# Issuing the first load ahead of the program's opening barrier in a ReLU-and-row-sum kernel

## The chip, the cores and the metric

The kernel runs on one core of one Trainium2 chip. The metric is the device time of one execution in microseconds (us), as the median of several runs. "The span" is the time from the first to the last instruction of the profiled execution; it is shorter than the measured time of the same execution, by 1.66 us in the profiled run of the kernel before (162.37 - 160.71). SyncE issues all loads and stores, ACT is the scalar engine, DVE the vector engine, POOL is GpSimd. A load's issue is SyncE's instruction that starts it; its lead is the time from the start of the issue to its first packet of data; it has landed when its semaphore has its full count.

The time before the change was 162.47 us (three runs, 162.46 to 162.50).

## The reference

```python
x = np.random.randn(32, 512, 1024).astype(np.float32)   # batch, seq, dim

def reference(x):
    relu_x = np.maximum(x, 0)
    return np.sum(relu_x, axis=-1).astype(np.float32)
```

The kernel reads 67.1 MB once, and writes 16,384 sums (0.07 MB).

## The kernel before

The rows are spread over 128 partitions, 128 rows of 1024 numbers on each. Seven big loads ("chunks") of 16 rows for each partition (8.39 MB) go in turn into three buffers, followed by a tail of smaller loads. SyncE issues the first three loads at once and each later one when DVE has finished with its buffer. ACT applies ReLU in place, and DVE sums.

```python
    sp, act, dve = nc.sync, nc.scalar, nc.vector

    tb = NBIG % NB                       # NBIG = 7 chunks, NB = 3 buffers
    for c in range(NBIG + 1):
        if c >= NB:
            sp.wait_ge(s_dve, 3 * (c - NB + 1))
        if c < NBIG:
            g, j = CHUNKS[c]
            sp.dma_start(out=buf[:, c % NB, :, :], in_=xv[g][:, j : j + BIG, :]).then_inc(
                s_in[c], 16
            )
    # ... the tail: loads of 8, 4, 2, 1/2 and 1/2 rows for each partition; the big store ...

    for c in range(NTWO):                # NTWO = 6 chunks are computed so
        b, steps = c % NB, STEPS if c < NTWO - 1 else MIXED
        act.wait_ge(s_in[c], 16)
        # ... two rows of the sixth chunk on DVE alone ...
        for i, n in enumerate(steps):    # STEPS = 4, 5 and 7 rows
            t = buf[:, b, r : r + n, :]
            act.activation(t, t, AF.Relu).then_inc(s_act, 1)
            dve.wait_ge(s_act, 3 * c + i + 1)
            dve.tensor_reduce(
                out=res[:, c * BIG + r : c * BIG + r + n], in_=t, axis=X, op=ALU.add
            ).then_inc(s_dve, 1)
            r += n
    # ... the last chunk and the tail, row by row on ACT and DVE; the small store ...
```

None of this is the first thing that the program does. The framework puts an opening before it: POOL fills four small constants, the four other engines announce their arrival at a barrier (a `DRAIN` instruction that increments one semaphore), and POOL, when it has reached its own `DRAIN` behind the constants, waits for these four arrivals and releases all by a second semaphore. In SyncE's stream of instructions the arrival and the wait for the release stand ahead of the first load.

## Time and profile before

| quantity | value | where it stands |
|---|---|---|
| time, span | 162.47 us, 160.7 us | runs, page |
| share of the load queue in 16 DMA engines' time | 97.4% | page, part 3 |
| busy DVE, ACT | 76%, 63% of the span | page, part 1 |
| first load issued | 0.73 us | timeline |
| first ReLU starts (load 0 has landed) | 22.61 us | timeline |
| second ReLU of a new chunk starts | 41.94 us, 19.33 us later | timeline |

Lines of the profile's page of the kernel before: the busy times of the engines, the DMA queue (packets, MB, share of the time of 16 engines) and the traffic with HBM.

```profile
span 160.7 us, 145 instructions
DVE 122.0 (76%) x56; ACT 101.0 (63%) x55; POOL 0.2 (0%) x4
...
q1 hardware_dynamic: 2160, 67.18, 97.4%
HBM read 67.11 MB, written 0.07 MB: 418 GB/s over the span
```

No compute engine is near full (76% and 63%), and the DMA engines are (97.4%). The waits of the kernel before say the same: who waited, for whom, and for how long (total us, times, longest).

```profile
ACT buf L118 <- DMA buf<-in_x_dram: 47.1, 6, 20.6
DVE res L120 <- ACT buf L118: 34.3, 10, 26.3
ACT buf L98 <- DMA buf<-in_x_dram: 9.7, 5, 6.6
```

ACT waits for data and DVE waits for ACT. Chunks follow each other at 19.33 us, or 8.39 MB / 19.33 us = 434 GB/s.

The timeline of the kernel before, its first 46 us (start, duration, engine, line, operation; in brackets the idle time before it and what ended that). "SPq L72 ... x4" merges the issues of loads 0 to 3, so its 43.92 us are the stretch from the first to the fourth.

```profile
0.23 0.10 POOL L169 MEMSET const-float32-0.0<- 128x1 f32 x1 [0.23 <-issue]
...
0.72 1.28 ACT L118 ACT_TABLE_LOAD   x1 [0.72 <-PEq L169]
0.73 43.92 SPq L72 DMA_DIRECT2D buf<-in_x_dram  x4
22.61 14.04 ACT L118 ACTIVATE buf<-buf 128x4096 f32<-128x4096 f32 x3 [20.60 <-DMA buf<-in_x_dram]
26.25 9.85 DVE L120 TENSOR_REDUCE res<-buf 128x4 f32<-128x4096 f32 x2 [26.25 <-ACT buf L118]
...
41.94 7.97 ACT L118 ACTIVATE buf<-buf 128x4096 f32<-128x4096 f32 x2 [5.29 <-DMA buf<-in_x_dram]
```

No load is issued until 0.73 us. The merged views leave the barrier out, since its instructions are not counted as work. The trace's single records have them (ns from the span's start, duration, engine):

```
   0    7  SyncE   DRAIN             arrival at the barrier
 304  181  POOL    DRAIN             its own, behind the four constants
 529   17  POOL    EVENT_SEMAPHORE   four arrivals are in
 607   17  POOL    EVENT_SEMAPHORE   release
 649   17  SyncE   EVENT_SEMAPHORE   passes
 731  383  SyncE   DMA_DIRECT2D      issue of load 0
1165  427  SyncE   DMA_DIRECT2D      issue of load 1
1751       DMA     first packet of data
```

SyncE arrives first of all engines and then does nothing for 0.65 us. It waits for POOL, whose own `DRAIN` ends at 0.49 us: POOL's records start at 0.14 us, and its four constants, which load 0 doesn't use, take from 0.24 to 0.44 us.

### The profile page before, as it was taken

What the parts mean: (1) busy time and instruction counts of PE and PEld (TensorE: products, weight loads), DVE (VectorE), ACT (ScalarE), POOL (GpSimd) and SP (SyncE); (2) the same over time, 40 slices, a digit from 0 to 9 for tenths busy, and PEclk for the clock granted to TensorE, in tenths of its full rate; (3) what the DMA queues carried; (4) which work ended last, traced back from release to release, by engine and by line L of the source; (5) the groups of instructions that cost most, each with busy time, mean ns of one, the idle gap of its engine ahead of it and who ended that gap; (6) DMA issues with size and microseconds to landing.
All of it is one profiled execution on the core that took longest, in us unless ns stands there. A gap on an engine that the chain in (4) does not pass through costs nothing.

```text
span 160.7 us, 145 instructions
## 1 busy us (share of the span) xinstructions
DVE 122.0 (76%) x56; ACT 101.0 (63%) x55; POOL 0.2 (0%) x4
## 2 busy tenths in 40 slices
DVE  0000004998969898898969989699899999598995
ACT  3000039991599907997099951999329980496972
POOL 0000000000000000000000000000000000000000
DMA  8969969969969969969969969969969969899993
GB/s 261 522 261 522 522 261 522 522 261 522 522 261 522 522 261 522 522 261 522 522 261 522 522 261 522 522 261 522 522 261 522 506 277 522 367 416 391 418 399 113
DMA packets 2160, 67.18 MB, mean 418 GB/s; under 512 B 496, under 2 KB 496, under 8 KB 880
## 3 DMA queue, kind: packets, MB, share of 16 engines
q1 hardware_dynamic: 2160, 67.18, 97.4%
HBM read 67.11 MB, written 0.07 MB: 418 GB/s over the span
## 4 chain that ended last, share of the span: by engine, by line
DMA 69%; ACT 18%; DVE 10%; SPq 1%; issue 0%
DMA buf<-in_x_dram 69%; ACT buf L118 17%; DVE res L120 9%; SPq L78 1%; ACT buf L98 0%; DVE last L101 0%; SPq L72 0%
## 5 line engine op out<-in xcount | busy, mean ns | idle before, releaser
L120 DVE TENSOR_REDUCE res<-buf 128x4 f32<-128x4096 f32 (+3 forms) x18 | 100.4, 5604 | 34.3 <-ACT buf L118 34.3
L118 ACT ACTIVATE buf<-buf 128x4096 f32<-128x4096 f32 (+3 forms) x18 | 80.8, 4553 | 47.1 <-DMA buf<-in_x_dram 47.1
L98 ACT ACTIVATE buf<-buf 128x1024 f32<-128x1024 f32 (+1 forms) x18 | 18.4, 1021 | 9.7 <-DMA buf<-in_x_dram 9.7
L101 DVE TENSOR_SCALAR_CACHE_REDUCE buf<-buf 128x1024 f32<-128x1024 f32 x18 | 21.0, 1215 | 2.7 <-DMA buf<-in_x_dram 2.5
L98 ACT ACTIVATION_READ_ACCUMULATOR buf<-buf 128x1 f32 x18 | 3.4, 186 | 0.0
L118 ACT ACT_TABLE_LOAD x1 | 1.3, 1283 | 0.7 <-PEq L169 0.7
L101 DVE DVE_READ_ACCUMULATOR buf<-buf 128x1 f32 x18 | 1.5, 83 | 0.0
L101 DVE TENSOR_SCALAR_CACHE_REDUCE last<-last 128x513 f32<-128x513 f32 x1 | 0.7, 690 | 0.2 <-ACT buf L98 0.2
L169 POOL MEMSET const-bfloat16-1.0<- 128x1 bf16 x1 | 0.1, 102 | 0.0
L169 POOL MEMSET const-uint8-127<- 128x1 uint8 x1 | 0.1, 102 | 0.0
L169 POOL MEMSET const-float32-0.0<- 128x1 f32 x1 | 0.1, 99 | 0.2 <-issue 0.2
L169 POOL MEMSET const-float32-1.0<- 128x1 f32 x1 | 0.1, 99 | 0.0
L101 DVE DVE_READ_ACCUMULATOR last<-last 128x1 f32 x1 | 0.1, 83 | 0.0
## 6 DMA issues: line engine op xcount, KB each, us to landing
buf<-in_x_dram SPq DMA_DIRECT2D x1, 4096.0 KB, 26.7
buf<-in_x_dram SPq DMA_DIRECT2D x1, 2048.0 KB, 31.2
buf<-in_x_dram SPq DMA_DIRECT2D x1, 1024.0 KB, 33.2
buf<-in_x_dram SPq DMA_DIRECT2D x1, 512.0 KB, 34.0
buf<-in_x_dram SPq DMA_DIRECT2D x1, 256.0 KB, 34.2
last<-in_x_dram SPq DMA_DIRECT2D x1, 256.0 KB, 34.3
buf<-in_x_dram SPq DMA_DIRECT2D x7, 36.3
out_dram<-res SPq DMA_DIRECT2D x1, 56.0 KB, 10.6
```

The lines of the kernel that those rows point to most:

```text
L78: sp.dma_start(out=buf[:, tb, r : r + n, :], in_=xv[-1][:, r : r + n, :]).then_inc(s_in[NBIG + i], 16)
L98: return act.activation(t, t, AF.Relu, accum_out=acc)
L101: return dve.tensor_scalar(out=t, in0=t, scalar1=0.0, scalar2=None, op0=ALU.max, op1=ALU.add, accum_out=acc)
L118: act.activation(t, t, AF.Relu).then_inc(s_act, 1)
L120: dve.tensor_reduce(out=res[:, c * BIG + r : c * BIG + r + n], in_=t, axis=X, op=ALU.add).then_inc(s_dve, 1)
L169: nc = _bacc.Bacc("TRN2", target_bir_lowering=False, num_devices=1)
```

## The change

The intent is to start the load stream at once. The instruction that issues load 0 is built as before, and then taken from the end of the instruction list and put ahead of SyncE's arrival. It writes one buffer and one semaphore that nothing ahead of the barrier touches, and the output is correct.

```diff
     tb = NBIG % NB
+    code = nc.main_func.blocks[0].instructions
+    arrival = next(
+        i
+        for i, ins in enumerate(code)
+        if ins.engine == mybir.EngineType.SP and type(ins).__name__ == "InstDrain"
+    )
     for c in range(NBIG + 1):
         # ... as before ...
             sp.dma_start(out=buf[:, c % NB, :, :], in_=xv[g][:, j : j + BIG, :]).then_inc(
                 s_in[c], 16
             )
+        if c == 0:
+            code.insert(arrival, code.pop())
```

## The prediction

> **What bounds the kernel now.** The load stream. The page gives queue 1 a 97.4% share of the span (67.11 MB read, 418 GB/s over the span). In the DMA packet records data packets run from 1.75 us to 157.92 us without a gap. The landings of the big loads are 19.35 us apart (8.39 MB each, 433 GB/s, worked out). The vector engine (76% busy) and the scalar engine (63%) wait for data: 47.1 + 9.7 us and 34.3 us in the table of waits. The chain of waits (DMA 69%) also walks through ACT and DVE, which release buffers, but that release is not tight: load 3 is issued when chunk 0 is reduced at 44.3 us, while load 2 lands only at about 61 us, so some 17 us of work is always queued. So what moves the stream's start moves every landing equally, and the end (last landing, 157.7 us, two short operations, the small store) follows.
>
> **What the change removes, adds, moves.** Before, in the timeline, SyncE's arrival at the barrier is the first instruction of the span (0.00 us, 7 ns). GpSimd's four memsets and its own arrival end near 0.49 us, GpSimd gathers at 0.53 and releases at 0.61, SyncE passes at 0.65, and the first load's issue starts at 0.73 us (383 ns long). Its first packet starts 1.02 us after that issue starts. The barrier thus stands wholly ahead of the stream. After the change the issue takes the place of the arrival, at about 0.00 to 0.06 us, and the first packet should start near 1.05 us of the same clock. Gain at the start: 0.67 to 0.73 us.
>
> **What it costs elsewhere.** SyncE reaches the barrier about 0.43 to 0.50 us later. GpSimd gathers at 0.53 us anyhow, so the release moves by 0 to 0.1 us. Behind it stand the table load of ACT (1.28 us, needed only at 22 us) and loads 1 and 2, which have about 19 us of slack behind load 0. So this costs nothing. [...]three loads being issued 0.43 to 0.48 us apart. So the arrival after the load should not wait for 8 MB.
>
> **Predicted time.** Nearly the whole gain survives, since the stream has no idle time that could absorb it: 162.47 - 0.69 = 161.78 us, 0.4% faster, so "same" at 2%. Range 161.6 to 162.05 us. Faster by over 2%: 0.005; within 2%: 0.99; slower by over 2%: 0.005.
>
> **What the profile would show.** First load's issue at about 0.0 us; the first landing's consumer (the first ACT activation, now 22.61 us) at about 21.9 us; activations still 19.35 us apart; the span near 160.0 us; loads 1 and 2 issued at about 0.7 to 0.8 and 1.2 us, not after 20 us.
>
> **What would make it wrong.** (a) The arrival waits until the load's data has landed: then load 1 is issued after 22 us, the stream has a hole of about 1 us, and the time is unchanged or up to 0.5 us worse. (b) The first issue is slower when it comes straight after the launch, which eats part of the 0.69 us. (c) The measured time, which is 1.7 us longer than the span, starts where the first instruction does and hides part of the gain.

## The result, and the profile after

| | before | after | difference |
|---|---|---|---|
| time, median (6 runs each) | 162.47 us | 161.53 us | 0.94 us |
| range of the runs | 162.19 to 162.53 | 161.42 to 161.65 | |
| span of the profiled run | 160.71 us | 159.91 us | 0.80 us |

The ratio is 0.9947, with a 95% interval of 0.9934 to 0.9960. Ratios in this document are the mean time of one kernel's runs over the mean of the other's in the same rounds, so not quite the ratio of the medians: here the means differ by 0.865 us and the medians by 0.94.

The page of the changed kernel, the same lines (line numbers in the source moved by 8 to 10):

```profile
span 159.9 us, 145 instructions
DVE 122.0 (76%) x56; ACT 101.0 (63%) x55; POOL 0.2 (0%) x4
...
q1 hardware_dynamic: 2160, 67.18, 97.9%
HBM read 67.11 MB, written 0.07 MB: 420 GB/s over the span
```

The work is the same to the tenth of a us; only the share of the queue rose, because the stretch without data at the start is shorter (1.01 us against 1.75). The waits of the changed kernel:

```profile
ACT buf L128 <- DMA buf<-in_x_dram: 46.3, 6, 19.7
DVE res L130 <- ACT buf L128: 33.5, 10, 25.5
ACT buf L108 <- DMA buf<-in_x_dram: 9.7, 5, 6.6
```

ACT's waits for data shrank by 0.8 us, DVE's for ACT by 0.8 us, and the longest wait of each, the one for chunk 0, gave all of it (20.6 to 19.7 and 26.3 to 25.5, rounded). The timeline of the changed kernel, its first 46 us:

```profile
0.00 43.86 SPq L80 DMA_DIRECT2D buf<-in_x_dram  x4
...
0.79 1.28 ACT L128 ACT_TABLE_LOAD   x1 [0.79 <-PEq L179]
21.82 14.04 ACT L128 ACTIVATE buf<-buf 128x4096 f32<-128x4096 f32 x3 [19.75 <-DMA buf<-in_x_dram]
25.46 9.85 DVE L130 TENSOR_REDUCE res<-buf 128x4 f32<-128x4096 f32 x2 [25.46 <-ACT buf L128]
...
41.13 7.98 ACT L128 ACTIVATE buf<-buf 128x4096 f32<-128x4096 f32 x2 [5.27 <-DMA buf<-in_x_dram]
```

Load 0 is issued at 0.00. ACT's table load, which stands behind the barrier, starts 0.06 us later than before (0.786 against 0.725 us in the single records). Everything from the first ReLU on is 0.8 us earlier, at the same spacing. The single records of the changed kernel's opening:

```
   0  383  SyncE   DMA_DIRECT2D      issue of load 0
 300  181  POOL    DRAIN
 431  132  SyncE   DRAIN             arrival (7 ns long before the change)
 589   17  POOL    EVENT_SEMAPHORE   four arrivals are in
 667   17  POOL    EVENT_SEMAPHORE   release
 709   17  SyncE   EVENT_SEMAPHORE   passes
 791  332  SyncE   DMA_DIRECT2D      issue of load 1
1010       DMA     first packet of data
```

The first packet comes 0.741 us sooner (1.751 to 1.010), and each of the thirteen loads lands 0.79 to 0.82 us sooner, load 0 included. So the gain is complete when load 0 has landed and nothing of it is lost over the 138 us that follow. What is to be settled is whether the earlier start is really the whole cause, whether the barrier still costs anything, and what the difference between 0.73 (the issue), 0.80 (the span) and 0.94 us (the medians) is.

### The profile page after: what moved, and what is told of

The parts are those of the page before. It is cut to its first block, busy times and chain, and to the rows that moved or that the text cites. A ratio compares the mean times of both kernels' runs of the same rounds, so it can differ in the third digit from the quotient of the medians.

```text
span 159.9 us, 145 instructions
## 1 busy us (share of the span) xinstructions
DVE 122.0 (76%) x56; ACT 101.0 (63%) x55; POOL 0.2 (0%) x4
## 4 chain that ended last, share of the span: by engine, by line
DMA 69%; ACT 18%; DVE 10%; SPq 1%; issue 0%
DMA buf<-in_x_dram 69%; ACT buf L128 18%; DVE res L130 10%; SPq L88 1%; ACT buf L108 0%; DVE last L111 0%
## 5 line engine op out<-in xcount | busy, mean ns | idle before, releaser
L130 DVE TENSOR_REDUCE res<-buf 128x4 f32<-128x4096 f32 (+3 forms) x18 | 100.4, 5604 | 33.5 <-ACT buf L128 33.5
```

Source lines behind the costliest of these rows:

```text
L130: dve.tensor_reduce(out=res[:, c * BIG + r : c * BIG + r + n], in_=t, axis=X, op=ALU.add).then_inc(s_dve, 1)
```

## The experiments

The theory is: time = time of the first load's issue + a constant. Rivals are that the late release of the barrier costs a part (or its lateness matters elsewhere), that any early DMA would do because the first one warms something up, that the landing of load 0 and not the stream counts, and that part of the 0.94 us is scatter. The variants of one call ran on one chip, beside runs of the kernel before on the same chip.

### Once more, and a third time: how large is the gain?

The edit is none; the changed kernel was timed again.

> The changed kernel once more, timed in more rounds beside its variants. Theory (the stream starts about 0.74 us earlier, nothing else counts): 0.65 to 0.90 us below the kernel before, so a ratio near 0.995; span about 159.9 us. Rival (part of the 0.94 us between the two medians of the first result is scatter between runs): nearer 0.75 than 0.94 us. If the gain is well over 0.85 us, something besides the earlier start is faster too.

> The changed kernel a third time, beside the two others on one chip: a ratio of 0.995 to 0.996 to the kernel before, 0.65 to 0.90 us.

| | before, mean (runs) | changed, mean (runs) | gain | ratio, 95% interval |
|---|---|---|---|---|
| the first result | 162.40 us (6) | 161.54 us (6) | 0.865 us | 0.9947 (0.9934 to 0.9960) |
| again | 162.28 us (9) | 161.62 us (5) | 0.661 us | 0.9960 (0.9947 to 0.9972) |
| third | 162.29 us (11) | 161.52 us (6) | 0.768 us | 0.9955 (0.9940 to 0.9969) |

Over all runs the means are 162.31 us (26 runs) and 161.56 us (17 runs), a gain of 0.757 us. The first 0.94 us was a difference of medians on the lucky side. The earlier issue, 0.731 us, lies inside all three intervals (0.65 to 1.07, 0.45 to 0.86 and 0.50 to 0.97 us), so the timings show no further gain.

### A barrier that opens late, without and with the change

Four fills of a scratch tile on POOL, put ahead of its arrival, hold the barrier shut for longer, by a time D. Their result is not used. The same edit was made to the kernel before and to the changed kernel.

```diff
+    scratch = nc.alloc_sbuf_tensor("scratch", [P, 4, 512], fp32)
+    ops = nc.main_func.blocks[0].instructions
+    for k in range(4):
+        nc.gpsimd.memset(scratch[:, k, :], 0.0)
+        ins = ops.pop()
+        at = next(                       # POOL's own DRAIN
+            i for i, o in enumerate(ops)
+            if o.engine == mybir.EngineType.Pool and type(o).__name__ == "InstDrain"
+        )
+        ops.insert(at, ins)
```

> The kernel before, with four memsets of 128x512 on GpSimd put ahead of its arrival at the barrier, so that the barrier opens later; their results are not used. How long they take is not known from the traces[...], D. Theory (the barrier stood wholly ahead of the stream): the release and the first load's issue move by D, and the time grows by D, to within 0.15 us. Rival (the barrier only matters in part, or the measured time doesn't count what lies ahead of the first load): less than D.

> The changed kernel with the same four memsets ahead of GpSimd's arrival. Theory: the barrier still opens D later, but the first load streams for some 20 us meanwhile, so the time is that of the changed kernel (161.5 us) within 0.15 us, and D plus about 0.8 us less than its twin without the change. Rival (the barrier still costs something behind the first load): part of D shows.

The timeline of the kernel before with the slow barrier:

```profile
0.36 1.91 POOL L67 MEMSET scratch<- 128x512 f32 x4
2.56 1.28 ACT L130 ACT_TABLE_LOAD   x1 [2.56 <-PEq L181]
2.57 1.32 SPq L84 DMA_DIRECT2D buf<-in_x_dram  x3
24.32 14.04 ACT L130 ACTIVATE buf<-buf 128x4096 f32<-128x4096 f32 x3 [20.47 <-DMA buf<-in_x_dram]
```

The timeline of the changed kernel with the slow barrier:

```profile
0.00 44.03 SPq L92 DMA_DIRECT2D buf<-in_x_dram  x4
...
0.36 1.91 POOL L67 MEMSET scratch<- 128x512 f32 x4
2.56 1.28 ACT L140 ACT_TABLE_LOAD   x1 [2.56 <-PEq L191]
21.99 14.04 ACT L140 ACTIVATE buf<-buf 128x4096 f32<-128x4096 f32 x3 [18.14 <-DMA buf<-in_x_dram]
```

The barrier opens equally late in both, since ACT's table load starts at 2.56 us in both. Without the change the first issue moved from 0.731 to 2.567 us, that is by D = 1.84 us, and the time from 162.40 to 164.06 us, by 1.66 us (ratio 1.0103, 1.0088 to 1.0118, or 1.43 to 1.92 us). That is 0.18 us short of D in the medians, slightly outside the 0.15 us expected, but D lies inside the interval; the scatter is looked at below. With the change the time is 161.46 us (ratio 0.9944, 0.9929 to 0.9959), as for the changed kernel without the slow barrier. The twins differ by 2.60 us, against 1.84 + 0.8 expected. So the barrier was paid for in full before the change, and after it a barrier three and a half times as long (2.56 us against 0.72 to ACT's table load) costs nothing. It also shows that the measured time counts what happens ahead of the first load.

### Between the arrival and the wait

The load is put behind SyncE's arrival, so that the arrival isn't late.

```diff
-            code.insert(arrival, code.pop())
+            code.insert(arrival + 1, code.pop())
```

> The first load is put after SyncE's arrival at the barrier but still before its wait for the release, so SyncE arrives on time and GpSimd gathers at about 0.53 us as before the change. Theory: issue starts at about 0.05 to 0.07 us instead of 0.00, so the gain is about 0.06 us smaller than that of the changed kernel (161.6 us), and the release comes at about 0.61 us, not 0.67. Rival (the 60 ns later release of ACT, DVE and loads 1 and 2 costs something): as fast as the changed kernel or faster.

The timeline of this variant:

```profile
0.08 1.45 SPq L80 DMA_DIRECT2D buf<-in_x_dram  x3
...
0.72 1.28 ACT L128 ACT_TABLE_LOAD   x1 [0.72 <-PEq L179]
21.95 3.62 ACT L128 ACTIVATE buf<-buf 128x4096 f32<-128x4096 f32 x1 [19.94 <-DMA buf<-in_x_dram]
```

The release is back at its old time (0.72 us for ACT's table load), and the issue is at 0.08 us. The median is 161.68 us, against 161.62 us for the changed kernel; the ratio to before is 0.9960 for both. The two means are equal (161.62 us), and the runs of one kernel spread over 0.3 to 0.6 us, so this run doesn't resolve 0.06 us, and doesn't decide between theory and rival. What decides against the rival are the variants with a much later release: 1.77 us later above, and 0.94 us later below.

### All three first loads ahead of the barrier

```diff
-        if c == 0:
-            code.insert(arrival, code.pop())
+        if c < 3:
+            code.insert(arrival + c, code.pop())
```

> Loads 0, 1 and 2 all ahead of the barrier. Theory (only the start of the stream counts): the release of ACT and DVE comes about 0.9 us later still (near 1.5 us), and the time is that of the changed kernel within 0.15 us (161.5 us). Rival (an early load 1 helps too, or the late release of ACT's table load and DVE costs): a difference of 0.3 us or more either way. It also shows whether SyncE's arrival waits for data that is under way: if it did, the release would come after 20 us.

The timeline of this variant:

```profile
0.00 1.33 SPq L80 DMA_DIRECT2D buf<-in_x_dram  x3
...
1.73 1.28 ACT L128 ACT_TABLE_LOAD   x1 [1.73 <-PEq L179]
21.92 3.62 ACT L128 ACTIVATE buf<-buf 128x4096 f32<-128x4096 f32 x1 [18.91 <-DMA buf<-in_x_dram]
```

The barrier opens 0.94 us later than in the changed kernel (ACT's table load at 1.73 against 0.79 us), and the median is 161.61 us against 161.62. An early load 1 brings nothing that these runs resolve (load 0 took 20.90 us from its first packet to its landing), and neither does the late release cost anything. SyncE's arrival took 125 ns (1.38 to 1.51 us) with three loads of 8.39 MB issued and the first packet moving since 1.01 us, so it doesn't wait for their data.

### A small dummy load ahead of the barrier, load 0 behind it

The kernel before, with this ahead of its loop (`arrival` is found as in the change; a wait for `s_warm` stands at the end):

```diff
+    warm = nc.alloc_sbuf_tensor("warm", [P, 16], fp32)
+    s_warm = nc.alloc_semaphore("s_warm")
+    sp.dma_start(out=warm[:, :], in_=xv[0][:, 0, 0:16]).then_inc(s_warm, 16)
+    code.insert(arrival, code.pop())
```

> The kernel before with a dummy load of 8 KB (its data is not used) ahead of the barrier; load 0 stays behind it. Rival theory (the first DMA of a program pays a warm-up, which the change takes ahead of the barrier; so any early DMA would do): the lead of load 0 from issue to first packet falls well below 1.0 us, and the time falls by some tenths of a us. Theory (only the start of load 0 counts): load 0 is issued at about 0.73 to 0.80 us with a lead of about 1.0 us, and the time is that of the kernel before within 0.15 us (162.3 to 162.5 us).

The timeline of this variant:

```profile
0.00 0.37 SPq L75 DMA_DIRECT2D warm<-in_x_dram  x1
...
0.78 1.28 SPq L82 DMA_DIRECT2D buf<-in_x_dram  x3
22.63 3.62 ACT L128 ACTIVATE buf<-buf 128x4096 f32<-128x4096 f32 x1 [20.57 <-DMA buf<-in_x_dram]
```

The time is 162.27 us, 162.17 for the kernel before (ratio 1.0005, 0.9990 to 1.0019). The lead of load 0 was 0.95 us instead of 1.02. Most of the difference is in the issue itself, which took 332 ns here and 383 ns before; from its end to the first packet it was 0.62 and 0.64 us. If there is a warm-up, it is worth less than 0.1 us; the rival falls. It is load 0 that has to be early.

### The wrong load ahead of the barrier

Load 1 is put ahead of the barrier, and load 0 stays behind it.

```diff
-        if c == 0:
+        if c == 1:
             code.insert(arrival, code.pop())
```

> Load 1 ahead of the barrier in place of load 0. Theory: the stream starts as early, but chunk 0, which is computed first, lands second, at about 41.1 us; its buffer is free only at about 62.8 us, when load 2 has landed at about 60.5 us; so the stream has a hole of 2.3 us plus the lead of 1.0 us, and the time is about 164.9 us, worse than before. If only the start of the stream counted, whichever load it is: 161.5 us.

The time is 169.06 us, 6.66 us slower than before and 4.2 us more than I expected. The chain of waits of this variant, shortened (start, duration, what):

```profile
0.79 40.40 DMA buf<-in_x_dram
...
41.22 14.05 ACT buf L128 x3
...
55.29 76.61 DVE res L130 x13
131.90 2.27 DVE buf L111 x4
134.17 12.98 DVE res L130 x3
147.15 15.49 DVE buf L111 x27
...
165.39 0.61 DVE last L111 x2
```

The chain is now DVE from 55 us to the end. DVE's first operation, in this variant's timeline:

```profile
44.86 9.85 DVE L130 TENSOR_REDUCE res<-buf 128x4 f32<-128x4096 f32 x2 [44.86 <-ACT buf L128]
```

Busy time in four stretches of 20 us of the same variant (stretch, its length, busy DVE, ACT and POOL with their counts, clock, DMA share, GB/s):

```profile
0.00:20.00 20.00, 0.00 (x0) 1.28 (x1) 0.20 (x4) 1.00 1.00 419
...
60.00:80.00 20.00, 20.00 (x4) 20.00 (x5) 0.00 (x0) 1.00 0.89 367
80.00:100.00 20.00, 20.00 (x5) 17.17 (x4) 0.00 (x0) 1.00 0.97 419
100.00:120.00 20.00, 20.00 (x5) 14.04 (x3) 0.00 (x0) 1.00 0.97 419
```

In the first 20 us the stream runs as in the changed kernel (419 GB/s), and there is a hole in it later (367 GB/s between 60 and 80 us): no data packet from 60.18 to 63.89 us, 3.7 us where 3.3 were expected. But DVE is busy almost without a pause. I had reckoned with the buffers alone and forgotten DVE: it needs 122.0 us, and in the changed kernel it idles only about 11 us after its first instruction (33.5 - 25.5 us waiting for ACT, and 2.5 + 0.2 us in small waits). Here it starts at 44.86 us instead of 25.46, 19.4 us late. Of that, 11 us can be absorbed; 19.4 - 11 = 8.4 us are left, 161.5 + 8.4 = 169.9 us by this sum, and 169.06 us was measured. The single records give it closer, since DVE's busy time is itself not the same in both, 122.0 us in the changed kernel and 120.6 us here: from DVE's first operation to the end of its last are 132.96 us in the changed kernel and 121.13 us here, so 11.8 us were absorbed and 7.6 us are left, 169.1 us. So here an early start of the stream is worth something only if the data that is needed first comes first.

### A smaller first load

Two variants of the changed kernel cut load 0 in two, both pieces ahead of the barrier, and ACT waits for 32 instead of 16 for chunk 0. The first piece has 1 row for each of 128 partitions in one variant, and all 16 rows of 16 partitions in the other.

```diff
-            sp.dma_start(out=buf[:, c % NB, :, :], in_=xv[g][:, j : j + BIG, :]).then_inc(...)
+            for r, n in ((0, 1), (1, 15)) if c == 0 else ((0, BIG),):          # by rows
+                sp.dma_start(out=buf[:, c % NB, r : r + n, :],
+                    in_=xv[g][:, j + r : j + r + n, :]).then_inc(s_in[c], 16)
...
+            for p, q in ((0, 16), (16, P)) if c == 0 else ((0, P),):           # by partitions
+                sp.dma_start(out=buf[p:q, c % NB, :, :],
+                    in_=xv[g][p:q, j : j + BIG, :]).then_inc(s_in[c], 16)
... each piece is put ahead of the arrival as before ...
```

> The first load cut in two, 1 row of 4 KB for each partition and then the other 15, both ahead of the barrier. Theory: the start of the stream is all that counts, so if a smaller first load has a shorter lead from issue to first packet (0.84 us for the small store at the end, 1.01 us for the big load), the time falls by up to 0.17 us below the changed kernel; if the lead is the same for every size, no change[...]. Rival (the time hangs on the landing of load 0 and not on the stream's start): no change whatever the lead does.

> The changed kernel with load 0 cut by partitions: 16 partitions of 64 KB first, then the other 112, both ahead of the barrier. If the issue time or the lead grows with the number of rows (128 in every load so far), the first packet comes sooner than 0.99 us and the time falls below the changed kernel by as much[...]; if not, no change (161.5 to 161.7 us).

Cut by rows, the first packet came 1.014 us after the issue, against 0.992 us for the whole load, and the median is 161.56 us against 161.62: no change. Cut by partitions, the first packet again came at 1.014 us, so 16 partitions instead of 128 made no difference to the lead either. But this variant took 183.07 us (ratio 1.129, 1.127 to 1.132), 21 us more than before, which nobody expected. Its first two stretches of 20 us:

```profile
0.00:20.00 20.00, 0.00 (x0) 1.28 (x1) 0.20 (x4) 1.00 1.06 200
20.00:40.00 20.00, 0.00 (x0) 0.00 (x0) 0.00 (x0) 1.00 0.95 226
```

The same stretches of the changed kernel in its third run:

```profile
0.00:20.00 20.00, 0.00 (x0) 1.28 (x1) 0.20 (x4) 1.00 1.00 419
20.00:40.00 20.00, 13.86 (x3) 14.04 (x3) 0.00 (x0) 1.00 0.97 419
```

The DMA engines are busy (DMA shares of 1.06 and 0.95), and the stream runs at half its rate until load 0 is in (200 and 226 GB/s against 419). The first piece, 1.05 MB on 16 partitions, took 11.2 us from first packet to landing, or 94 GB/s (9.8 us to the end of its last packet, or 107 GB/s). The second piece, 112 partitions, is alone between 20 and 40 us and still slow, at 226 GB/s. The packet records show where the slowness sits: a packet of 64 KB took 2.42 us in the loads of 128 partitions once the stream ran, 7.7 to 9.2 us in the first piece and 2.9 to 4.9 us (4.3 on average) in the second, after the first had landed. The packets were slower; the stream had no pause. The cause of the slowness is open for both pieces.

### Where the scatter comes from

The profiles show more than a timing can. From the records of the profiled executions (us), all but the wrong load and the cut by partitions, where the stream itself was disturbed:

| kernel | issue of load 0 | issue to first packet | first packet to landing of load 0 | that landing to end of span | issue to end |
|---|---|---|---|---|---|
| before | 0.73 | 1.02 | 20.83 | 138.13 | 159.98 |
| changed | 0.00 | 1.01 | 20.78 | 138.12 | 159.91 |
| changed, again | 0.00 | 0.99 | 20.93 | 138.14 | 160.07 |
| changed, third | 0.00 | 1.00 | 20.89 | 138.11 | 159.99 |
| between | 0.08 | 1.00 | 20.85 | 138.10 | 159.95 |
| three first | 0.00 | 1.01 | 20.90 | 138.13 | 160.03 |
| cut by rows | 0.00 | 1.01 | 20.86 | 138.13 | 160.00 |
| dummy first | 0.78 | 0.95 | 20.87 | 138.20 | 160.02 |
| before, slow barrier | 2.57 | 1.00 | 20.73 | 138.14 | 159.87 |
| changed, slow barrier | 0.00 | 1.01 | 20.95 | 138.14 | 160.10 |

The last column is the theory in one number. The first load is issued anywhere from 0.00 to 2.57 us, and the end comes 159.87 to 160.10 us after that. The 0.23 us of scatter arise while load 0 is coming in (20.73 to 20.95 us); from its landing on all agree within 0.05 us, but for the dummy's variant, which has an additional wait at its end and is 0.06 us above the next highest. This also tells what the 0.80 us of the two spans are: 0.73 us of earlier issue, and 0.07 us by which those two executions differed in the landing of load 0 and the lead. What makes the landing vary is open.

## Why the prediction was right

- **What bounds the kernel.** Right. The stream has no idle time after its start (the loads' packets run without a gap from 1.75 to 157.92 us before, and from 1.01 to 157.10 us after), and all thirteen landings moved alike, by 0.79 to 0.82 us. The slow-barrier twins show it the hard way: D = 1.84 us more ahead of the stream cost 1.66 us, and behind it nothing.
- **The gain at the start.** "0.67 to 0.73 us" for the issue: 0.731 us, since the issue took exactly the place of the arrival. The packets moved by 0.741 us.
- **The barrier behind it.** "The release moves by 0 to 0.1 us": 0.06 us. "So this costs nothing": shown by the variants with the release 0.94 and 1.77 us later, at 161.61 and 161.46 us.
- **The arrival doesn't wait for data.** Right, though before the run it was an estimate, with nothing but the spacing of three issues (0.43 to 0.48 us) behind it. The arrival took 0.13 us and ended at 0.56 us, load 1 was issued at 0.79 us, not after 20, and load 0 landed at 21.79 us.
- **The time.** 161.78 us was forecast, and 161.53 us measured. The size was 0.69 us, and over 26 and 17 runs it is 0.757 us. The mis-sized term is the midpoint of 0.67 to 0.73 for the issue: it measured 0.73. The rest is scatter. When the range of 161.6 to 162.05 us was drawn, only three runs of the kernel before were on record, and they lay within 0.04 us; the same kernel spread from 162.01 to 162.67 us later. The median of the first result lies 0.07 us below the lower edge as an absolute number; 0.9947 of 162.47 us is 161.61 us, just inside. The range should have reached down to some 161.4 us.
- **What could have made it wrong.** (a) didn't happen, as said in the point on the arrival. (b) The lead at the launch was 1.01 us, and 1.02 us before: no slower. (c) The measured time exceeds the span by 1.66 us before (162.37 - 160.71, the profiled runs) and 1.63 us after (161.54 - 159.91): nothing is hidden.
- One sentence leaves a condition out: "what moves the stream's start moves every landing equally, and the end (...) follows". It takes for granted that chunk 0 stays the first to land. In the wrong-load variant the stream started as early, but chunk 0 landed 19.4 us later, more than the 11 to 12 us that DVE could absorb, and DVE set the end. Smaller shifts of chunk 0 alone were not tried. (The last load landed at 158.41 us, not at 157.7, which is the last that ACT waits for; nothing in the forecast hangs on it.)

## What to carry to other kernels

In a kernel bound by its load stream, look at what stands ahead of the first load's issue, to the ns and with the barrier's own records: here all of it was paid in full, and the load, which needs nothing from the barrier, could go ahead of it. Only the load that is consumed first had to be moved, and the gain was the time by which its issue came earlier and no more (0.73 us, 0.45%). Moving another load there, or cutting the first one by partitions to start sooner, cost 7 and 21 us.
